# Moving parts built by VectorE alone, evictions spread over steps, and bias masks made as signs on ScalarE, in a hand-ordered transformer block

## The chip, the cores and the metric

The kernel runs on one core of one Trainium2 chip. The metric is the device time of one execution in microseconds (us). The core's engines are named as in the profile: PE (TensorE, matmuls), PEld (PE's weight loads), DVE (VectorE), ACT (ScalarE), POOL (GpSimd) and SP (SyncE, which here only issues DMAs). Each of them executes its own instructions strictly in order; semaphores hold an instruction back until what it needs is there. An engine's queue of issued DMAs appears with a q behind its name (ACTq, SPq). PSUM has eight banks of 128x512 float32, in which PE accumulates.

## The reference

One layer of a streaming encoder over 512 positions with 2048 channels, all in float32:

```python
h = rmsnorm(x, norm_gain)
proj = h @ w_in
(aq, ak, av, az, iq, ik, iw, rq, rk, rv, rz, ga, gb) = jnp.split(proj, SPLIT_POINTS, axis=-1)
...
# mixer A: for each query the 128 keys with the best index score
index = jnp.einsum('bqsh,bqh->bqs', jax.nn.relu(score), w_c)
_, sel = lax.top_k(index, topk)
bias = rel_table[t5_bucket(pos_sel - pos_c[:, :, None])]
logits = jnp.einsum('bqhd,bqkhd->bqkh', q_c, k_sel) * scale + bias
...
# mixer B: chunkwise retention over rq, rk (rotary) and rv, group norm
merged = sigmoid(ga) * (a_out @ w_a_out) + sigmoid(gb) * (b_out @ w_b_out)
r = x + merged @ w_o
return rmsnorm(r + (p_i @ w_ple) * sigmoid(r @ w_ple_gate), final_gain)
```

## The kernel before

**Precision.** A float32 product is made of three matmuls in the faster fp32r type: each operand is the sum of a high part (its value rounded to fp32r) and a low part (what is left), and high x high, high x low and low x high are accumulated. For a weight tile of 128x1024 (`wraw`, or `wt` for some), ACT makes the high part `wh` (line 153) and DVE subtracts it to get the low part `wl` (line 158). Every weight passes through ACT and DVE so, in `split_to`.

**Products in pairs.** Most of the projections are done two weight blocks at a time with a scheme of seven products in place of eight (Strassen's, in Winograd's form): `block_pair` and `block_wide_pair` set up the seven weight combinations. Some combinations are sums, which an accumulating DMA issued by POOL makes (line 119) or DVE (line 160). `gemm_pair` multiplies: for each of the seven products (units 0 to 6) there is a high run of eight matmuls 512 wide and a low run of eight matmuls 256 wide (line 283), in the order of `RUNS`: high 0, high 1, low 0, low 1, high 2, high 3, low 2, low 3, low 4, high 4, high 5, low 5, low 6, high 6. Four banks (`ps_p`, `ps_v`, `ps_q`, `ps_r`) accumulate. `SPLIT_AT` says ahead of which run a unit's split is recorded.

**The moving parts.** The other operand of those products is made once, from the normalised input `xn`, by `combos` (line 291). For each of eight steps `k` and each of seven combinations (`PRODUCTS`: s3, a11, a12, s4, s2, a22, s1) there is a tile of 128x512: its left half `LO` is the high part and comes from ACT (line 299), its right half `HI` is the low part. Four of the combinations need sums (`sums`, lines 310 to 316): four subtractions of 128x256. Before the change these are made by POOL (`adder=pool`), as are the low parts of s1, s4 and a22 (line 301); the other low parts are made by DVE. Tiles of the input carry names that begin with h in the profile (`hs`, `ha`), those of a later use, on `merged`, begin with m (`ms`). As all 56 tiles don't fit, twelve of them (`X_AWAY = 4` steps times three combinations) are stored to DRAM by SP when made and loaded again by `x_load` before they are needed.

**Passes of values.** `values` makes a half of rv: it multiplies 16 steps by four row tiles into four banks (`ps_vn`), in groups of three matmuls (lines 755 to 757). After it, `normal` (line 764) takes each bank out of PSUM with a scaling on ACT, and ACT issues the store of it (line 892). There are two such passes. They end at 148 and at 194.5 us. `values_pair` then makes both halves of av by the scheme of seven products, into banks `ps_vv`, `ps_vp`, `ps_vq` and `ps_vr` (two of each; lines 947 to 949); `copy` (ACT) and `out` take the banks out: `value_out` (line 896) makes the sum `av` on DVE (line 899), `split` makes the high part `avh` on ACT (line 734) and the low part `avl` on DVE (line 735), and ACT issues their stores 10 or 12 steps later (line 906). `last()` does so for four results at once at the end of the pair.

**Order.** No scheduler runs: the order of the instructions on each engine is the order in which the program records them. Each small group of matmuls (three in the passes, two in a gemm pair) ends with `step()`, a tick:

```python
def later(n, f):
    ...
    heapq.heappush(soon, (tick[0] + n, tick[1], f))

def step():
    tick[0] += 1
    while soon and soon[0][0] <= tick[0]:
        heapq.heappop(soon)[2]()
    f = todo.popleft() if todo else None
    if f is not None:
        f()
    elif bg and tick[0] % state["rate"] == 0:
        bg.popleft()()
```

Work for the other engines is so laid between the matmuls: what was put off with `later` falls due at its tick; else one entry of the list `todo` is recorded; else, each `rate`-th tick, one of the list `bg`. `BG_RATES` holds the rates of the stages. In `bg` stand, in this order, the steps of `combos`, the sixteen top-k rounds (`topk_round`, MAX8 at line 650 and MATCH_REPLACE8 at line 651, in three widths), and the bias masks.

**Around the change.** At 72 to 122 us the first rv pass and the index scores run (`index_score`: score matmuls at lines 610 and 611, relu on ACT at line 613, a weighted sum on DVE at line 620), with the split of the index queries (`iq_split`, lines 463 and 464) and the rotary tables (`f_turns` and `f_rope2`: `ang` on DVE at line 580, sine `st` and cosine `ct` on ACT at lines 587 and 590). The pair of av ends at 272 us and the first gemm pair begins (the gates; its `out` makes `e_t` at line 250 and `go` at line 967).

**Bias masks.** The bias depends on the bucket of the relative position. It is written as a first value plus a sum of differences, each times a mask "relative position at least threshold". A mask is 128 rows (32 buckets for each of four queries) by up to 512 keys in float16. DVE makes them with a comparison (line 666, 128 of them), `bias_mm` multiplies them with the table's differences `d2` (two float16 parts), and `bias_out` scales back by `d_back`.

**Space.** The U pool holds 69 tiles of 128x512 float32 (`U_BUFS`), given out in turn: a new tile takes the slot that was released, and its first writer waits until the slot's last reader (which may be a store) is done.

Of the kernel before, what the change touches and what calls it, by code (L numbers as in the profile page):

```python
# [9 lines left out]
F32 = mybir.dt.float32  # L10
# [25 lines left out]
def block_kernel(tc, xT, pT, posb, posq, w_in, w_v, w_ik, w_a, w_b, w_o, w_ple, w_gate,  # L36
# [4 lines left out]
    with contextlib.ExitStack() as ctx:  # L41
# [249 lines left out]
        def combos(lo, hi, name, keep=None, adder=dve, low={}):  # L291
# [5 lines left out]
            def parts(n, k, src, sign=1.0):  # L297
                t = U(name + n, F32R)
                act.activation(t[:, LO], src, AF.Copy, scale=sign)
                if sign > 0:  # L300
                    low.get(n, dve).tensor_sub(t[:, HI], src, t[:, LO].bitcast(F32))
# [81 lines left out]
        tb = cp.tile([128, 65], F32, name="tb")  # L383
# [150 lines left out]
        def f_pos():  # L534
# [11 lines left out]
            dve.max(d8, da)  # L546

# [6 lines left out]
        def f_table2():  # L554
# [7 lines left out]
            dve.tensor_scalar(d_back.bitcast(I32), e.bitcast(I32), 1.0, -14.0 * 2 ** 23, op0=OP.mult, op1=OP.add)  # L562
# [32 lines left out]
        todo.extend(N3 * 3 + [f_sum] + N3 * 3 + [f_rnat] + N3 * 3 + [f_bcast, None, f_keys1] + N3 * 3 + [f_keys2] + N3 * 2 + [f_keys3] + N3 * 2)  # L595
# [32 lines left out]

        for m in range(2):
            index_tile(m, ix[m])  # L630
# [28 lines left out]
        def bias_mask(b, i):  # L659

            t, gs = b
# [4 lines left out]
            dve.tensor_scalar(bias_e[b][:, ln * i:ln * i + ln], relf[:, :ln], thr[:, q:q + 1], None, op0=OP.is_ge)  # L666
# [28 lines left out]
        x_away = [(n, k) for k in range(X_AWAY) for n in PRODUCTS[4:]]  # L695
        hd = dp.tile([len(x_away), 128, L], F32, name="hd")
        x_at = {nk: hd[i] for i, nk in enumerate(x_away)}
        xn = {}

        def xn_load(k):  # L700
            for i in (k, k + 8):
                xn[i] = U("xn")
                sp.dma_start(xn[i], xT[:, i, :])

        def xn_norm(k):
            for i in (k, k + 8):
                dve.scalar_tensor_tensor(xn[i], xn[i], ng[:, i:i + 1], R["b"], op0=OP.mult, op1=OP.mult)

        Xh, h_step = combos(lambda k: xn[k], lambda k: xn[k + 8], "h", lambda n, k: x_at.get((n, k)), pool,
                            {n: pool for n in ("s1", "s4", "a22")})  # L710
# [172 lines left out]
        def x_load(s):  # L883
            if s >= KT - len(x_away) and x_wanted:
# [4 lines left out]
        for i in range(2):  # L889
            pss = values(u_rv[i], "rv", x_load if i else lambda s: None)  # L890
            for t, ps in enumerate(pss):
                act.dma_start(rd[i, t], normal(ps, "rv", t))
        state["rate"] = BG_RATES[2]


        def value_out(i, t, f, x, y):
# [8 lines left out]
            for j, v in vs:  # L905
                later(10 + 2 * (j % 2), lambda j=j, v=v: act.dma_start(vd[i, j], v))

        def values_pair(ids):
# [25 lines left out]
            for n, b in enumerate("vpqrpvp"):  # L934
# [20 lines left out]
        state["rate"] = BG_RATES[3]  # L955
# [29 lines left out]
        state["rate"] = BG_RATES[5]  # L985
# [408 lines left out]
BG_RATES = (2, 3, 5, 24, 16, 8)  # L1394
X_AWAY = 4
# [10 lines left out]
def _layout(x, p, positions, w_in, norm_gain, w_a_out, w_b_out, w_o, ret_gn_gain,  # L1406
# [88 lines left out]
```

## Time and profile before

| what | value |
|---|---|
| time, median of 3 runs | 1680.68 us |
| the runs | 1679.4, 1680.68 and 1682.84 us |
| profiled execution, its own time | 1680.43 us |
| profiled execution, its span | 1678.7 us |
| mean granted PE clock | 0.998 |
| DMA over the span | 204 GB/s, 343.26 MB |
| POOL's issue of accumulating DMAs of w_in (line 119) | 120, 106.1 us busy |
| wl on DVE (line 158) | 459, 565.4 us busy, 1241 ns each |
| wh on ACT (line 153) | 459, 474.3 us busy, 1043 ns each |

The profile has one profiled execution. In a row of instructions stand the start, the duration, the engine, the line, the operation, output <- inputs by the program's names, the shapes, the count, and in brackets how long the engine stood idle before and what released it. In a row of groups stand the count, the busy time, the mean ns of one, and the idle time ahead of them. PE's records overlap a little, as its matmuls are pipelined. The span is 1.7 us shorter than the profiled execution's own time.

### The profile page before, as it was taken

How to read it: one execution, taken by the hardware profiler on the slowest of the kernel's cores; microseconds unless marked ns; L12 is line 12 of the kernel's file. 1: busy time of each engine (PE TensorE's matmuls, PEld its weight loads, DVE VectorE, ACT ScalarE, POOL GpSimd, SP SyncE). 2: the span in 40 equal slices, each digit the busy share in tenths (PEclk: the TensorE clock that was granted, in tenths of full speed). 3: DMA queues.
4: the chain of work that ended last, by engine and by line, in shares of the span. 5: the costliest groups of instructions: out<-in, count | busy, mean ns of one | idle time of the engine just before them, and what ended most of it. 6: DMA issues, size and time to landing. Idle time of an engine off the chain costs nothing.

```text
span 1678.7 us, 24639 instructions
## 1 busy us (share of the span) xinstructions
PE 1660.2 (99%) x9160; PEld 1441.5 (86%) x9160; DVE 1300.1 (77%) x1984; ACT 880.0 (52%) x1296; POOL 284.3 (17%) x288
## 2 busy tenths in 40 slices
PE   9999999999999999999999999999999999999997
PEld 7988788888888888888888888888888888888896
DVE  7798988988988887887887777787668887864453
ACT  7465544555555555555555555566633445463342
POOL 2116611111111111111331111100000111112222
PEclk9999999999999999999999999999999999999999
DMA  7427989788788788788998888898466788733222
GB/s 288 127 91 236 321 234 268 174 218 218 181 210 220 178 232 230 168 229 227 248 235 219 218 223 218 247 373 284 162 210 193 196 216 218 208 108 101 88 63 101
DMA packets 125577, 343.26 MB, mean 204 GB/s; under 512 B 13713, under 2 KB 25873, under 8 KB 125457
## 3 DMA queue, kind: packets, MB, share of 16 engines
q1 hardware_dynamic: 90400, 235.22, 41.5%
q0 software_dynamic: 23680, 85.99, 28.1%
q10 hardware_dynamic: 11376, 20.47, 3.4%
q8 instruction: 72, 1.18, 0.3%
q14 instruction: 49, 0.39, 0.1%
HBM read 300.21 MB, written 41.42 MB: 204 GB/s over the span
## 4 chain that ended last, share of the span: by engine, by line
PE 89%; DVE 4%; ACT 2%; issue 2%; POOL 2%; DMA 1%; ACTq 0%; SPq 0%; POOLq 0%; DVEq 0%
PE ps_p L283 23%; PE ps_v L283 15%; PE ps_r L283 8%; PE ps_q L283 7%; PE ps_w L213 3%; PE ps_w L214 3%; PE ps_w L215 3%; PE ps_pg L215 3%; PE ps_pg L213 3%; PE ps_pg L214 3%; PE ps_iq L213 1%; PE ps_iq L215 1%; PE ps_iq L214 1%; DVE wl L158 1%; ACT wh L153 1%
## 5 line engine op out<-in xcount | busy, mean ns | idle before, releaser
L158 DVE TENSOR_TENSOR wl<-wraw,wh 128x1024 fp32r<-128x1024 f32 (+2 forms) x459 | 565.4, 1241 | 156.6 <-ACT wh L153 155.4
L153 ACT ACTIVATE wh<-wraw 128x1024 fp32r<-128x1024 f32 (+2 forms) x459 | 474.3, 1043 | 257.9 <-DVE wraw L160 120.3
L119 POOL DMA_DIRECT2D wraw<-w_in x120 | 106.1, 962 | 644.1 <-DVE mk L666 245.3
L283 PE MATMUL ps_p<-hs,wh 128*128 128x512 f32 x640 | 161.1, 394 | 0.0
L246 ACT ACTIVATE e<-ps_p 128x512 f32<-128x512 f32 x144 | 86.1, 598 | 136.7 <-PE ps_p L283 134.3
L283 PEld LDWEIGHTS ps_p<-hs,wh 128*128 128x128 f32 x640 | 114.9, 189 | 21.3 <-issue 0.7
L283 PE MATMUL ps_p<-hs,wl 128*128 128x256 f32 x640 | 92.1, 284 | 1.6 <-DVE wl L158 1.6
L283 PEld LDWEIGHTS ps_p<-hs,wl 128*128 128x128 f32 x640 | 83.0, 192 | 2.1 <-DVE wl L158 2.0
L283 PE MATMUL ps_r<-hs,wh 128*128 128x512 f32 x320 | 79.9, 392 | 1.3 <-ACT wh L153 1.3
L119 POOL DMA_DIRECT2D wraw<-w_o x24 | 21.1, 945 | 348.5 <-DVE wl L158 316.5
L283 PE MATMUL ps_q<-ha,wh 128*128 128x512 f32 x320 | 80.1, 392 | 0.0
L283 PE MATMUL ps_v<-ha,wh 128*128 128x512 f32 x320 | 80.0, 392 | 0.0
L283 PE MATMUL ps_p<-ha,wh 128*128 128x512 f32 x320 | 79.3, 390 | 0.0
L283 PE MATMUL ps_v<-hs,wh 128*128 128x512 f32 x320 | 79.0, 389 | 0.0
L215 PE MATMUL ps_pg<-rh,wl 128*128 128x512 f32 x192 | 74.8, 390 | 0.0
L214 PE MATMUL ps_pg<-rl,wh 128*128 128x512 f32 x192 | 74.7, 389 | 0.0
L213 PE MATMUL ps_pg<-rh,wh 128*128 128x512 f32 x192 | 74.7, 389 | 0.0
L967 DVE TENSOR_TENSOR go<-e_t 128x256 f32<-128x256 f32 x160 | 68.0, 425 | 6.8 <-DMA bd<-go 1.2
L283 PEld LDWEIGHTS ps_r<-hs,wh 128*128 128x128 f32 x320 | 59.6, 188 | 15.8 <-ACT wh L153 2.9
L283 PEld LDWEIGHTS ps_p<-ha,wh 128*128 128x128 f32 x320 | 59.9, 188 | 12.9 <-issue 0.5
L283 PEld LDWEIGHTS ps_v<-hs,wh 128*128 128x128 f32 x320 | 60.1, 188 | 12.5
L283 PEld LDWEIGHTS ps_v<-ha,wh 128*128 128x128 f32 x320 | 59.5, 188 | 12.1
(409 smaller groups left out, 3739.9 us busy)
## 6 DMA issues: line engine op xcount, KB each, us to landing
wraw<-w_in SPq DMA_DIRECT2D x172, 512.0 KB, 5.3
wraw<-w_in POOLq DMA_DIRECT2D x120, 512.0 KB, 8.0
wraw<-w_v SPq DMA_DIRECT2D x32, 512.0 KB, 4.2
wraw<-w_o SPq DMA_DIRECT2D x32, 512.0 KB, 4.8
wraw<-w_o POOLq DMA_DIRECT2D x24, 512.0 KB, 7.0
wraw<-w_gate SPq DMA_DIRECT2D x24, 512.0 KB, 4.0
wraw<-w_b SPq DMA_DIRECT2D x16, 512.0 KB, 5.9
wraw<-w_a SPq DMA_DIRECT2D x16, 512.0 KB, 4.1
```

Source lines behind the costliest of these rows:

```text
L119: pool.dma_start(out=view(raw_tiles[r], nk, cols), in_=src[:, k0:k0 + nk, :], accum_op=OP.add)
L153: act.activation(h, raw, AF.Copy)
L158: dve.tensor_sub(l, raw, h.bitcast(F32))
L213: pe.matmul(o, h[:, k, w], a, start=(s == order[0]), stop=False)
L214: pe.matmul(o, h[:, k, w], b, start=False, stop=False)
L215: pe.matmul(o, l[:, k, w], a, start=False, stop=(s == order[-1]))
L246: act.activation(E[n], src, AF.Copy)
L283: pe.matmul(o[:, c], w[:, k], X[PRODUCTS[n]][k][:, c], start=(n < 4 and first and k == 0), stop=(ended[n] == 16), skip_group_check=True)
L967: dve.tensor_add(o[:, q], c0, c1)
```

## The change

It has five parts.

1. `combos` loses its arguments `adder` and `low`: the four sums of a step and all low parts are made by DVE. That moves 56 operations of 128x256 from POOL to DVE.
2. The steps of `combos` start earlier: step 0 is recorded by `x_first`, from an entry of `todo`, one part each six ticks from tick 4 on; steps 1 to 7 stand in `bg` ahead of twelve empty entries (`X_PAUSE`) and the top-k rounds. `X_AWAY` is 5, so fifteen tiles are stored and loaded again; `x_load` begins earlier (`s > 2`) and goes on in the pair of values.
3. The results of an rv pass are taken out of PSUM, and stored, three ticks apart (`later(3 * t, ...)`). The last four of the pair of values are made at ticks 6, 9, 14 and 21 after its end, with their stores 18 or 20 ticks behind.
4. The bias masks are ACT's Sign of the relative position plus a negated threshold, so +1 or -1 in place of 1 or 0. The table's differences are halved (the exponent in `d_back`), its first value is set to the mean of first and last, the thresholds lie half-way between integers, and the table has one more column for the signs.
5. `BG_RATES` has five values: 2 till the rv passes are done, 5 in the pair of values, 24 behind it, 16 from the masks on, 8 at the end.

```diff
-        def combos(lo, hi, name, keep=None, adder=dve, low={}):
+        def combos(lo, hi, name, keep=None):
...
-                    low.get(n, dve).tensor_sub(t[:, HI], src, t[:, LO].bitcast(F32))
+                    dve.tensor_sub(t[:, HI], src, t[:, LO].bitcast(F32))
...
-                adder.tensor_sub(t2[:, LO], x[:, LO], x[:, HI])
-                adder.tensor_sub(t1[:, LO], x[:, HI], y[:, HI])
-                adder.tensor_sub(t1[:, HI], x[:, LO], t1[:, LO])
-                adder.tensor_sub(t2[:, HI], y[:, LO], t1[:, HI])
+                dve.tensor_sub(t2[:, LO], x[:, LO], x[:, HI])
+                dve.tensor_sub(t1[:, LO], x[:, HI], y[:, HI])
+                dve.tensor_sub(t1[:, HI], x[:, LO], t1[:, LO])
+                dve.tensor_sub(t2[:, HI], y[:, LO], t1[:, HI])
...
-            dve.tensor_scalar(thr, thr, tb[:, 64:65], None, op0=OP.add)
+            dve.tensor_scalar(thr, thr, tb[:, 64:65], -1.0, op0=OP.add, op1=OP.mult)
...
-            dve.tensor_sub(dl, tb[:, 0:32], tb[:, 32:64])
+            dve.scalar_tensor_tensor(dl, tb[:, 32:64], tb[:, 65:66], tb[:, 0:32], op0=OP.mult, op1=OP.add)
...
-            dve.tensor_scalar(d_back.bitcast(I32), e.bitcast(I32), 1.0, -14.0 * 2 ** 23, op0=OP.mult, op1=OP.add)
+            dve.tensor_scalar(d_back.bitcast(I32), e.bitcast(I32), 1.0, -15.0 * 2 ** 23, op0=OP.mult, op1=OP.add)
...
-        todo.extend(N3 * 3 + [f_sum] + N3 * 3 + [f_rnat] + N3 * 3 + [f_bcast, None, f_keys1] + N3 * 3 + [f_keys2] + N3 * 2 + [f_keys3] + N3 * 2)
+        todo.extend(N3 * 3 + [f_sum] + N3 * 3 + [f_rnat] + N3 * 3 + [f_bcast, lambda: x_first(), f_keys1] + N3 * 3 + [f_keys2] + N3 * 2 + [f_keys3] + N3 * 2)
...
+        def x_steps(k):
+            load = [lambda: xn_load(k + 1)] if k < 7 else []
+            return load + [lambda: xn_norm(k)] + [lambda i=i: h_step(k, i) for i in range(X_STEPS)]
+        def x_first():
+            for i, f in enumerate([lambda: xn_load(0)] + x_steps(0)):
+                later(4 + 6 * i, f)
...
-            dve.tensor_scalar(bias_e[b][:, ln * i:ln * i + ln], relf[:, :ln], thr[:, q:q + 1], None, op0=OP.is_ge)
+            act.activation(bias_e[b][:, ln * i:ln * i + ln], relf[:, :ln], AF.Sign, bias=thr[:, q:q + 1])
...
-        bg.append(lambda: xn_load(0))
-        for k in range(8):
-            if k < 7:
-                bg.append(lambda k=k: xn_load(k + 1))
-            bg.append(lambda k=k: xn_norm(k))
-            bg.extend([lambda k=k, i=i: h_step(k, i) for i in range(X_STEPS)])
-
-        bg.append(lambda: state.update(rate=BG_RATES[1]))
-        for r in range(16):
-            for t in range(1, NT):
-                bg.append(lambda r=r, t=t: topk_round(t, r == 15))
-        bg.append(lambda: state.update(rate=BG_RATES[4]))
+        rounds = [lambda r=r, t=t: topk_round(t, r == 15) for r in range(16) for t in range(1, NT)]
+        for k in range(1, 8):
+            bg.extend(x_steps(k))
+        bg.extend([lambda: None] * X_PAUSE)
+        bg.extend(rounds)
+        bg.append(lambda: state.update(rate=BG_RATES[3]))
...
         def x_load(s):
-            if s >= KT - len(x_away) and x_wanted:
+            if s > 2 and x_wanted:
...
-            pss = values(u_rv[i], "rv", x_load if i else lambda s: None)
-            for t, ps in enumerate(pss):
-                act.dma_start(rd[i, t], normal(ps, "rv", t))
+            for t, ps in enumerate(values(u_rv[i], "rv", x_load if i else lambda s: None)):
+                later(3 * t, lambda i=i, t=t, ps=ps: act.dma_start(rd[i, t], normal(ps, "rv", t)))
...
-                later(10 + 2 * (j % 2), lambda j=j, v=v: act.dma_start(vd[i, j], v))
+                later(lag + 2 * (j % 2), lambda j=j, v=v: act.dma_start(vd[i, j], v))
...
-            def out(f, b, n, i, half):
+            def out(f, b, n, i, half, at=0, lag=10):
                 for j in range(2):
-                    value_out(i, 2 * half + j, f, banks[b][j], E[n][j])
+                    later(at + at // 2 * j, lambda j=j: value_out(i, 2 * half + j, f, banks[b][j], E[n][j], lag))
...
-                out(dve.tensor_sub, "p", "pv", 1, 1)
-                out(dve.tensor_add, "r", "e3", 1, 0)
+                out(dve.tensor_sub, "p", "pv", 1, 1, 6, 18)
+                out(dve.tensor_add, "r", "e3", 1, 0, 14, 18)
...
+                    x_load(8 * n + s + 4)
...
-BG_RATES = (2, 3, 5, 24, 16, 8)
-X_AWAY = 4
+BG_RATES = (2, 5, 24, 16, 8)
+X_AWAY = 5
+X_PAUSE = 12
...
-    t = np.zeros((128, 65), f32)
+    t = np.zeros((128, 66), f32)
...
-            if b:
-                t[32 * q + b, 32 + 8 * q:40 + 8 * q] = tab[ROW[b - 1]]
-        t[32 * q:32 * q + 32, 64] = [-1e9] + THR[1:] + [1e9]
+            t[32 * q + b, 32 + 8 * q:40 + 8 * q] = tab[ROW[b - 1]]
+        t[32 * q:32 * q + 32, 64] = [-1e9] + [i - 0.5 for i in THR[1:]] + [1e9]
+        t[32 * q:32 * q + 32, 65] = [1.0] + [-1.0] * 31
```

More of the change, by code (lines that the diff above doesn't have):

```diff
@@ L382, in block_kernel @@
         posq_i = cp.tile([128, 128], I32, name="posq_i")
-        tb = cp.tile([128, 65], F32, name="tb")
+        tb = cp.tile([128, 66], F32, name="tb")
         ones = cp.tile([128, 128], F32, name="ones")
@@ L627, in index_tile, with xn_load, xn_norm @@
                     todo.append(lambda s=s, t=t: index_score(2 * m + s, ix[s], t))
+        x_away = [(n, k) for k in range(X_AWAY) for n in PRODUCTS[4:]]
+        hd = dp.tile([len(x_away), 128, L], F32, name="hd")
+        x_at = {nk: hd[i] for i, nk in enumerate(x_away)}
+        xn = {}
+        def xn_load(k):
+            for i in (k, k + 8):
+                xn[i] = U("xn")
+                sp.dma_start(xn[i], xT[:, i, :])
+        def xn_norm(k):
+            for i in (k, k + 8):
+                dve.scalar_tensor_tensor(xn[i], xn[i], ng[:, i:i + 1], R["b"], op0=OP.mult, op1=OP.mult)
+        Xh, h_step = combos(lambda k: xn[k], lambda k: xn[k + 8], "h", lambda n, k: x_at.get((n, k)))
+        def x_steps(k):
[4 more added lines that the diff above has]
+                later(4 + 6 * i, f)
         for m in range(2):
@@ L693, in bias_banks @@
                 bias_out(b, ps)
[L695 to L710, printed above, removed]
-        bg.append(lambda: xn_load(0))
-        for k in range(8):
-            if k < 7:
-                bg.append(lambda k=k: xn_load(k + 1))
-            bg.append(lambda k=k: xn_norm(k))
-            bg.extend([lambda k=k, i=i: h_step(k, i) for i in range(X_STEPS)])
-        bg.append(lambda: state.update(rate=BG_RATES[1]))
-        for r in range(16):
-            for t in range(1, NT):
-                bg.append(lambda r=r, t=t: topk_round(t, r == 15))
-        bg.append(lambda: state.update(rate=BG_RATES[4]))
+        rounds = [lambda r=r, t=t: topk_round(t, r == 15) for r in range(16) for t in range(1, NT)]
[4 more added lines that the diff above has]
+        bg.append(lambda: state.update(rate=BG_RATES[3]))
         banks = [(t, tuple(range(8 * t + g, 8 * t + g + n))) for t, n in reversed(tuple(enumerate((4, 2, 1, 1))))
@@ L954, in block_kernel @@
         values_pair(u_av)
-        state["rate"] = BG_RATES[3]
+        state["rate"] = BG_RATES[2]
         sgb, sga, mbs = (dp.tile([16, 128, L], F32, name=n) for n in ("sgb", "sga", "mbs"))
@@ L984, in block_kernel @@
                 gate_pair(u_g[n], to(d[m:m + 2], AF.Sigmoid))
-        state["rate"] = BG_RATES[5]
+        state["rate"] = BG_RATES[4]
         for n, u in enumerate(u_rz):
```

4 lines of the change are left out of this document (2 added, 2 removed).

## The prediction

> **What bounds the kernel now.** First the page: the busy shares and the chain that ended last.
>
> ```profile
> span 1678.7 us, 24639 instructions
> PE 1660.2 (99%) x9160; PEld 1441.5 (86%) x9160; DVE 1300.1 (77%) x1984; ACT 880.0 (52%) x1296; POOL 284.3 (17%) x288
> PE 89%; DVE 4%; ACT 2%; issue 2%; POOL 2%; DMA 1%; ACTq 0%; SPq 0%; POOLq 0%; DVEq 0%
> ```
>
> TensorE (PE) is busy 99% of the span, and 89% of the chain is its own work. The change removes no matmul, so all it can win is the time in which PE waits. That is the second view, the waits of PE; the columns are the total in us, the times and the longest.
>
> ```profile
> PE ps_b L1368 <- POOL rl L1364: 3.5, 1, 3.5
> PE ps_p L283 <- DVE wl L158: 1.6, 2, 1.3
> PE ps_vv L948 <- DVE wl L158: 1.5, 2, 0.8
> PE ps_vv L947 <- ACT wh L153: 1.4, 1, 1.4
> ...
> PE ps_r L283 <- ACT wh L153: 1.3, 3, 0.6
> ```
>
> The first is the end of the kernel and stays. The other four hold 1.6 + 1.5 + 1.4 + 1.3 = 5.8 us, 0.35% of the span; those left out hold 1.4 at the very start and less behind it. So 5.8 is the most that the change can win by taking waits away. What it can lose has no such bound: weights are split into wh on ScalarE (ACT) and wl on VectorE (DVE), and whatever stands in these queues ahead of a split can become a new wait of PE. So I looked for the places where the change puts work in front of one.
>
> **Part B: the evictions of the rv passes, −3.4 us.** The timeline of ACT at the end of the second rv pass, where the pair of av begins:
>
> ```profile
> 194.54 0.67 ACT L764 ACTIVATE rv<-ps_vn,r_nat 128x512 f32<-128x512 f32 x1
> 195.24 0.33 ACTq L892 DMA_DIRECT2D rd<-rv  x1
> ...
> 198.97 2.01 ACT L153 ACTIVATE wh<-wt 128x1024 fp32r<-128x1024 f32 x2 [0.40 <-ACT rv L764]
> ```
>
> And that of PE, with one of its waits:
>
> ```profile
> 194.46 0.39 PE L949 MATMUL ps_vv<-wh,hs 128*128 128x512 f32 x1
> 194.68 0.39 PE L947 MATMUL ps_vv<-wh,hs 128*128 128x512 f32 x1
> 195.86 0.50 PE L948 MATMUL ps_vv<-wl,hs 128*128 128x512 f32 x1 [0.79 <-DVE wl L158]
> ```
>
> Four evictions, each with its store issued behind it, fill ACT from 194.54 to 198.97; only then comes the next wh. DVE's wl needs that wh, and the three ps_vv waits above follow (1.4 + 1.5 = 2.9 us). In the changed order the evictions stand three steps (nine matmuls, some 2 us at the 0.23 from one matmul's start to the next) apart, and the wh stand between them; 0.67 + 0.33 us fits into 2 us. The three waits go. A stall costs a little more than the wait shown: at that pace the one at 195.86 follows the one at 194.68 by 0.95 us too much, of which 0.79 is called a wait. I add that 0.16 for each of the three: 2.9 + 0.5 = 3.4. Bounds: −2.9 to −3.6.
>
> **Part A: the moving parts on DVE alone, +2.6 us.** Per step k seven operations of 128x256 (four sums, three low parts) go from POOL to DVE, 56 in all, and step 0 is made some 64 us into the kernel instead of after 105 us. The prices on DVE, by shape, DVE's load in the two stretches concerned (columns: busy PE, PEld, DVE, ACT, POOL), and two rows of its timeline:
>
> ```profile
> L301 DVE TENSOR_TENSOR hs<-t,hs 128x256 fp32r<-128x256 f32 x16 | 13.9, 890 | 0.0
> L301 DVE TENSOR_TENSOR ms<-t,ms 128x256 fp32r<-128x256 f32 x32 | 12.0, 417 | 0.0
> 72.50:99.00 26.50, 26.50 (x151) 25.29 (x150) 23.20 (x50) 17.90 (x33) 0.00 (x0) 1.00 0.38 120
> 99.00:118.00 19.00, 19.00 (x92) 16.04 (x91) 18.82 (x29) 9.78 (x19) 4.00 (x4) 1.00 0.28 77
> ```
>
> ```profile
> 103.58 1.41 DVE L580 SCALAR_TENSOR_TENSOR ang<-kk,ang 128x512 f32<-128x512 f32 x2
> ...
> 110.84 2.37 DVE L580 SCALAR_TENSOR_TENSOR ang<-kk,ang 128x512 f32<-128x512 f32 x2
> ```
>
> The same operation takes 0.42 us alone (ms) and 0.89 beside POOL (hs); L580 shows it too, 1.41 and 2.37. So the moved operations cost 56 x 0.42 = 23 us, and 16 x 0.47 = 7.6 come back at the hs row, 0.96 at L580, more at others like it. Where they fall is what counts. From 72.5 to 99 DVE has 26.50 − 23.20 = 3.3 us free; step 0 brings 7 x 0.42 = 2.9 and the normalisation, two operations of 128x512 with two inputs, 1.41 like the pair at 103.58: 4.3 us, so 1.0 too much. From 99 to 118 it has 0.18 free; six operations of step 1 bring 2.5, and 0.96 comes back at L580: 1.4 too much (0.18 taken off). DVE is 2.4 us late at 118, and 0.7 more if a fifth of the free 3.3 falls between dependent instructions, where nothing fits. Who waits for that: ACT works in order, and its casts of the sums stand ahead of the following rows.
>
> ```profile
> 117.10 1.28 ACT L587 ACT_TABLE_LOAD   x1
> ...
> 119.79 0.72 ACT L590 ACTIVATE ct<-ang,cs 128x512 f32<-128x512 f32 x1 [0.76 <-DVE ang L588]
> 120.42 0.47 ACT L613 ACTIVATE relu<-ps_is 128x384 f32<-128x384 f32 x1
> ```
>
> ```profile
> 121.31 0.40 PE L610 MATMUL ps_is<-ikh,tz 128*128 128x512 f32 x1
> ```
>
> ACT's ct at L590 waits for DVE's ang, the relu at 120.42 stands behind it, and the matmul at 121.31 writes the bank which that relu empties at 120.89 (four of the eight banks hold rv until the pass ends). The slack is 0.4 to 0.5 us: 2.4 + 0.7 − 0.5 = +2.6. Bounds: 0, if what comes back for POOL's absence leaves ang no later, and +3.5, with all seven operations of step 1 and a little more idle in it.
> The Trainium skill, page "SBUF — State Buffer", section "Who interferes with whom", says that a DVE instruction with two SBUF inputs and a GpSimd instruction that reads SBUF exclude one another for the whole instruction. The pair 0.89 and 0.42 agrees, and by that rule alone the change repays DVE for much of what it brings, and A would be 0. The rows of 99 to 118 speak against that, since only 0.96 us of POOL's cost is seen there.
>
> **Part C: the evictions of the pair of av passes, +5.2 us.** This is the large term. The pair ends at 271.9, and the first gemm pair follows; its matmuls on PE, and the wait:
>
> ```profile
> 282.10 1.12 PE L283 MATMUL ps_r<-hs,wl 128*128 128x256 f32 x8
> 284.52 1.22 PE L283 MATMUL ps_p<-hs,wl 128*128 128x256 f32 x8 [1.30 <-DVE wl L158]
> ```
>
> Eight wide matmuls take 8 x 0.23 = 1.82 us, eight narrow ones half as long, some 0.93. So unit 4's low part, due at 282.10 + 0.93 = 283.0, came at 284.5: the wait of 1.3, with its restart 1.5. Today the four last evictions stand in one block at the head of the gemm pair and their stores block ACT; the change puts them at steps 6, 9, 14 and 21, stores 18 steps behind. That wait goes: −1.5. Without it unit 4's high part starts at 284.0, unit 5's high at 285.8 and its low at 287.6. The prices of what now stands in front of unit 5:
>
> ```profile
> L158 DVE TENSOR_TENSOR wl<-wraw,wh 128x1024 fp32r<-128x1024 f32 x3 | 3.6, 1216 | 0.0
> L735 DVE TENSOR_TENSOR avl<-av,avh 128x512 fp32r<-128x512 f32 x3 | 1.9, 682 | 0.0
> L246 ACT ACTIVATE e<-ps_p 128x512 f32<-128x512 f32 x144 | 86.1, 598 | 136.7 <-PE ps_p L283 134.3
> 276.68 0.49 ACTq L906 DMA_DIRECT2D vd<-av  x1
> ```
>
> DVE's changed order from 272.3 on: a top-k round of 512 (two passes of 512 at avl's 0.68, 1.4), three wl and one weight sum (4 x 1.22 = 4.9), four av and two avl (6 x 0.68 = 4.1), 10.4 in all, with 1.7 for the handovers to ACT and back: the last eviction, r's second half, is done at 284.4. ACT casts its avh (0.6), then issues three stores (0.33 as for rd, to 0.49 each, 1.25), then makes unit 5's wh (1.05): 287.3 where 285.8 was due, 1.5 late. DVE is later still. Its last avl goes into a slot of the U pool that an earlier avh leaves, whose store is issued just before, about 285.0; in the changed order that avl carries a wait for a DMA. DVE stands until the store has landed (L), then come avl 0.68, the output's e_t 0.68, go 0.42 (256 wide, as ms) and unit 5's wl 1.22: ready at 285.0 + L + 3.0 = 288.0 + L, due 287.6. PE waits 0.4 + L, in place of the 1.5. L from the issue-to-landing rows of such stores:
>
> ```profile
> vd<-avh ACTq DMA_DIRECT2D x2, 256.0 KB, 2.6
> vd<-avh ACTq DMA_DIRECT2D x1, 256.0 KB, 6.3
> vd<-avl ACTq DMA_DIRECT2D x1, 256.0 KB, 8.5
> ```
>
> They are 2.6 for two issued alone (234 us), 6.3 for the first of a batch behind two weight loads (267 us), 8.5 in a batch (278 us). Nearest is 6.3: a first store, weight loads about. C = 0.4 + 6.3 − 1.5 = +5.2; with the others +1.5 and +7.4.
> The Trainium skill, page "DMA: Bandwidth & Descriptors", section "Anatomy of one DMA — SWDGE (gpsimd) path", puts some 2.0 us, mostly the receipt of the write, on every transfer, and the bytes at 436 GB/s on top; an estimate from that page is 2.6 us here. The quiet store agrees, the other two do not; by the page's figure the sum below would be +0.7, 1681.1.
>
> **Part D: masks on ACT, 0.** The masks' source row, and a window of their stage:
>
> ```profile
> L666 DVE TENSOR_SCALAR mk<-relf,thr x128: 275/410/1461, 502.3 to 1039.4; 128x512 f16<-128x512 f32 x32, 128x384 f16<-128x384 f32 x32, 128x256 f16<-128x256 f32 x32, 128x128 f16<-128x128 f32 x32
> 800.00:840.00 40.00, 40.00 (x254) 34.21 (x253) 33.43 (x44) 22.51 (x30) 13.55 (x14) 1.00 0.97 264
> ```
>
> Some 128 x 0.41 = 52 us leave DVE, where PE waits for nothing (none of the waits lies there), so they buy nothing. On ACT each costs at most the 0.60 of a 512-wide pass: 77 us over 537 us; ACT has 17.5 of 40 us free. The free time is what hides it; without it, one mask in ten ahead of a late wh makes 12.8 x 0.6 = +7.7. The rest: three more parts are stored and loaded again, six DMAs of 256 KB more on SP; no wait of PE names a load behind the start, so 0, and at an issue of 0.33 each at most +2.0. The table's extra column and the idle slots ahead of the top-k rounds add no work on PE.
>
> **Sum:** 1680.4 (the profiled execution's own time) − 3.4 + 2.6 + 5.2 = 1684.8. The median of the runs is 1680.7, 0.3 above the profiled one, so nothing is added. About 0.2% (3.4 us) is what a measurement of this kernel can tell from no change.
>
> **The rivals.**
> R1, no new wait: the slot that avl takes is free in time and ang no later. −3.4 − 1.5 = 1675.5. For it: DVE's total falls by some 40 us (52 − 23 + 7.6 and more) and ACT has room. Against it: 0.18 us free from 99 to 118. This is the other side, faster.
> R2, A holds, the store doesn't hold DVE: −3.4 + 2.6 − 1.5 = 1678.1, no measurable change. For it: the two stores issued alone landed in 2.6, and a store issued earlier than 285.0 frees the slot in time.
> R3, C holds, A doesn't: −3.4 + 5.2 = 1682.2, no measurable change.
> R4, masks come ahead of wh: the one in ten above in place of A, −3.4 + 5.2 + 7.7 = +9.5, 1689.9. For it: ACT works in order; against it, 17.5 of 40 us free.
> R5, the upper prices: −2.9 + 3.5 + 7.4 = +8.0, 1688.4.
> That the change doesn't do what it says: the spread evictions may still be queued behind each other, since DVE's order, not the steps, sets when av is made; then B alone falls away and the sum is 1688.2, counted with R5.
>
> **How the numbers follow.** Forecast 0.46 (its own range 1682 to 1688; 0.38 of it slower, 0.08 within 0.2%), R1 0.19 faster, R2 0.08 and R3 0.09 the same, R4 0.06 and R5 0.12 slower. Faster 0.19, same 0.25, slower 0.56. The range runs from R1 (1675.5) to just above R5, 1690.
>
> **What would show it.** B: no ps_vv wait near 195 to 200. A: a wait of ps_is near 121 for relu, 2 to 3 us, with DVE full from 99 to 118. C: no wait for unit 4's wl, but one of PE for unit 5's wl near 288, 6 to 7 us, and DVE idle at an avl released by a DMA of vd. D: no PE wait from 502 to 1039. Wrong is the forecast if the wait at unit 5 is under 3 us or the score matmuls don't wait.

## The result, and the profile after

The changed kernel takes 1685.35 us (median of 14 runs) beside 1681.22 us of the kernel before (14 runs). The ratio is 1.0022, with an interval of 1.0014 to 1.0030: slower by 0.2%. 1684.8 us had been forecast. The profiled execution has a span of 1683.2 us beside 1678.7, 4.5 us more. The total came out as forecast, but the terms behind it did not: one was far too large, and one of nearly the same size was missing. That they cancel is luck.

First the page's two top rows, then the waits of PE (total us, times, longest), those at start and end left out:

```profile
span 1683.2 us, 24616 instructions
...
PE 1660.9 (99%) x9160; PEld 1440.9 (86%) x9160; DVE 1254.7 (75%) x1912; ACT 932.7 (55%) x1424; POOL 228.5 (14%) x232
```

```profile
PE ps_r L283 <- ACT wh L153: 3.4, 4, 1.7
PE ps_v L283 <- ACT wh L153: 2.5, 2, 1.6
PE ps_v L283 <- DVE wl L158: 1.6, 1, 1.6
...
PE ps_is L611 <- ACT relu L614: 1.3, 1, 1.3
...
PE ps_p L283 <- DVE wl L158: 0.8, 1, 0.8
PE ps_is L611 <- DVE tz L464: 0.4, 1, 0.4
```

DVE has 45 us less to do and ACT 53 us more, mostly the masks. Neither shows in the time; PE's busy time is the same. All that counts is in the second fence. Sorted by place, with the 0.16 us that each wait costs beside its length:

| place | waits before | waits after | change | forecast |
|---|---|---|---|---|
| B, 194 to 200 us | 2.9 in 3 | none | -3.4 | -3.4 |
| A, 101 and 121 us | none | 1.7 in 2 | +2.0 | +2.6 |
| C, 282 to 289 us | 1.3 in 1 | 2.5 in 2 | +1.3 | +5.2 |
| D, 480 to 1090 us | 0.7 in 2 | 4.9 in 4 | +4.5 | 0 |

The changes add up to +4.4, and the spans differ by 4.5. These are the waits of one profiled execution of each kernel; in the other traces the same place differs by up to 3 us, as the experiments show. A place is named by the start of the last matmul ahead of the wait; the row of the matmul that waited has a later time.

**Place A.** The timelines of ACT and of PE, and DVE's load from 99 to 118 us (columns as in the prediction):

```profile
117.98 1.22 ACT L299 ACTIVATE hs<-t 128x256 fp32r<-128x256 f32 x3 [3.10 <-DVE t L313]
119.10 0.37 ACT L614 ACTIVATE relu<-ps_is 128x256 f32<-128x256 f32 x1
119.48 1.28 ACT L588 ACT_TABLE_LOAD   x1
...
122.80 0.47 ACT L614 ACTIVATE relu<-ps_is 128x384 f32<-128x384 f32 x1
```

```profile
123.32 0.50 PE L611 MATMUL ps_is<-ikh,tz 128*128 128x512 f32 x1 [1.30 <-ACT relu L614]
```

```profile
99.00:118.00 19.00, 18.64 (x89) 15.44 (x88) 18.75 (x33) 8.21 (x17) 0.00 (x0) 1.00 0.19 56
```

ACT stands 3.1 us at the casts of step 1's sums, which DVE, full all the time, makes late. The table load comes 2.4 us later than before (119.48; it was 117.10), the relu too, and PE waits for it: the forecast wait, 1.3 long in place of 2 to 3. The other wait, 0.4 at 101 us for the split of the index queries (`tz`), had not been forecast.

**Place C.** DVE, the store that it waits for with its time to landing, and PE:

```profile
282.99 0.41 DVE L676 MATCH_REPLACE8 isc<-m,isc 128x256 f32<-128x256 f32 x1
285.74 0.69 DVE L739 TENSOR_TENSOR avl<-av,avh 128x512 fp32r<-128x512 f32 x1 [2.34 <-DMA vd<-avh]
```

```profile
282.65 0.33 ACTq L909 DMA_DIRECT2D vd<-avh  x1
```

```profile
vd<-avh ACTq DMA_DIRECT2D x1, 256.0 KB, 3.0
```

```profile
285.18 2.14 PE L283 MATMUL ps_v<-ha,wh 128*128 128x512 f32 x8 [0.87 <-ACT wh L153]
288.87 1.22 PE L283 MATMUL ps_v<-ha,wl 128*128 128x256 f32 x8 [1.55 <-DVE wl L158]
```

The last avl waits for the store that frees its slot, as forecast. But the store is issued at 282.65, not 285.0, and lands in 3.0 us, not 6.3. PE waits 0.87 for unit 5's wh and 1.55 for its wl.

**Place D.** Here the prediction had nothing. The rows of the masks and of MAX8 give their times, first and last:

```profile
L692 ACT ACTIVATE mk<-relf,thr x128: 384/554/737, 531.1 to 1055.5; 128x512 f16<-128x512 f32 x32, 128x384 f16<-128x384 f32 x32, 128x256 f16<-128x256 f32 x32, 128x128 f16<-128x128 f32 x32
```

```profile
L675 DVE MAX8 m<-isc x48: 417/554/689, 203.2 to 519.4; 128x8 f32<-128x256 f32 x16, 128x8 f32<-128x384 f32 x16, 128x8 f32<-128x512 f32 x16
```

The masks start at 531.1, not at 502.3. The top-k rounds ahead of them start later, so fewer of them fall into the stages with the quick rates, and three more go at one each 24 steps: in the recorded order the first bias bank stands at step 1206, before at 1126. The first four of the eleven pairs of banks come 80 steps later, the last six 40. The banks are so at other places within the gemm pairs of 56 steps. What this does at 941 us, in the order of time: SP's timeline, its wait, POOL's and ACT's rows:

```profile
907.53 0.33 SPq L132 DMA_DIRECT2D wraw<-w_in  x1
918.54 3.96 SPq L715 DMA_DIRECT2D scr<-bev  x4
922.61 1.33 SPq L132 DMA_DIRECT2D wraw<-w_in  x1
```

```profile
SPq L715 <- ACT bev L711: 10.6, 1, 10.6
```

```profile
933.36 0.88 POOL L119 DMA_DIRECT2D wraw<-w_in  x1 [10.40 <-issue]
```

```profile
942.12 1.06 ACT L153 ACTIVATE wh<-wraw 128x1024 fp32r<-128x1024 f32 x1 [5.42 <-DMA wraw<-w_in]
```

SP issues in order. It reaches the store of a bias bank and stands 10.6 us, till ACT has taken the bank out of PSUM; the weight loads behind it come out from 922.6 on and take some 10 us to land, POOL adds the second half of one at 933.36, that lands 8.7 us later, and ACT's wh stands 5.4 us for it. The hold alone is not the difference, though: in the kernel before SP stands 10.5 us ahead of the same stores (at 905 us), and no wait of PE follows. What differs is which loads are due behind it. That the hold makes this wait is read from the chain; no run takes the hold away and leaves all else. At 1071 us ACT's wh waits for the landing of a bias store. The chain there:

```profile
1062.84 8.45 DMA scr<-bev
...
1071.37 0.33 ACTq L981 DMA_DIRECT2D zd<-go  x1
1071.79 1.06 ACT L153 ACTIVATE wh<-wraw 128x1024 fp32r<-128x1024 f32 x1 [4.39 <-DMA scr<-bev]
```

A bias store takes 8.45 us to land, ACT's issue of a gate's store waits for that landing (the program makes it wait for the semaphore which that store raises, beside the one for its data), and the wh behind it is late.

### The profile page after: what moved, and what is told of

It reads as the page before. It is cut to its first block, busy times and chain, and to the rows that moved or that the text cites. A ratio compares the mean times of both kernels' runs of the same rounds, so it can differ in the third digit from the quotient of the medians.

```text
span 1683.2 us, 24616 instructions
## 1 busy us (share of the span) xinstructions
PE 1660.9 (99%) x9160; PEld 1440.9 (86%) x9160; DVE 1254.7 (75%) x1912; ACT 932.7 (55%) x1424; POOL 228.5 (14%) x232
## 5 line engine op out<-in xcount | busy, mean ns | idle before, releaser
L692 ACT ACTIVATE mk<-relf,thr 128x512 f16<-128x512 f32 (+3 forms) x128 | 70.8, 553 | 19.6 <-DVE go L971 11.9
```

Source lines behind the costliest of these rows:

```text
L692: act.activation(bias_e[b][:, ln * i:ln * i + ln], relf[:, :ln], AF.Sign, bias=thr[:, q:q + 1])
```

## The experiments

All ratios are to the kernel before, run on the same chips.

**Who makes the masks, and when.** The first two start from the changed kernel.

```diff
-            act.activation(bias_e[b][:, ln * i:ln * i + ln], relf[:, :ln], AF.Sign, bias=thr[:, q:q + 1])
+            dve.tensor_scalar(bias_e[b][:, ln * i:ln * i + ln], relf[:, :ln], thr[:, q:q + 1], None, op0=OP.is_ge)
...
```

> The changed kernel with its bias masks made by VectorE again, with the table as before; all else, the time of the masks too, stays. The changed kernel waits 5.6 us on TensorE in the stage of the masks at 707, 941, 950 and 1070 us, in places where the kernel before doesn't wait. Theory 1 (the masks stand in ScalarE's queue ahead of weight casts and evictions): these four waits go, about 1680 us. Theory 2 (the whole bias work comes 80 steps later and so at other places in the gemm pairs, where its stores meet the weight loads): the waits at 941 and 1070 stay whoever makes the masks, about 1685 us. The waits at 121 and 283 to 288 us stay in both.

Ratio 1.0011 (1.0002 to 1.0021). The waits of PE from 480 to 1090 us in this run:

```profile
PE ps_r L283 <- ACT wh L153: 2.2, 3, 1.6
PE ps_v L283 <- ACT wh L153: 1.9, 1, 1.9
PE ps_p L283 <- DVE wl L158: 0.2, 1, 0.2
```

4.3 of 4.9 us stay with the masks off ACT, the two large ones among them. Theory 1 falls for these. The time alone, between the two expectations, wouldn't have told.

```diff
         bg.append(lambda: state.update(rate=BG_RATES[3]))
+        bg.extend([lambda: None] * 2)
```

> The changed kernel with two empty slots of 16 steps ahead of the masks, which puts each bias bank one or two whole gemm pairs (56 steps each) after its place in the kernel before, so at the same place within a pair; the masks stay on ScalarE. Theory 1 (the masks in ScalarE's queue): waits of some 5 us stay in the stage, about 1685 us. Theory 2 (the place in the pair): they go, about 1680 us.

Ratio 0.9999 (0.9987 to 1.0010). The fifth of the eleven pairs of banks stands 72 steps after its old place, so not at the same place within a gemm pair; PE doesn't wait there. The waits at 707, 941, 950 and 1070 are gone, as theory 2 has it, but the profile has a new one at 679 us (3.1) and a small one after 840:

```profile
PE ps_r L283 <- ACT wh L153: 3.1, 1, 3.1
PE ps_v L283 <- DVE wl L158: 0.8, 1, 0.8
```

The chain behind the long one is of the kind seen at 941 us: SP stands at two stores ahead of weight loads, and ACT stands 3.9 us for a load that POOL issued at 661.87 and that landed 9.0 us later. And this wait costs more than its length. Behind it come eight wide matmuls, which elsewhere take some 2.0 us; then two windows, where the third number from the end is the granted clock of PE:

```profile
682.85 3.13 PE L283 MATMUL ps_r<-hs,wh 128*128 128x512 f32 x8 [3.12 <-ACT wh L153]
684.00:686.00 2.00, 2.00 (x7) 1.55 (x6) 1.97 (x3) 1.32 (x2) 0.00 (x0) 0.50 0.15 45
680.00:690.00 10.00, 7.15 (x40) 6.55 (x41) 8.18 (x11) 7.94 (x12) 0.00 (x0) 0.83 0.71 177
```

The clock is at half, and 10 us at 0.83 lose 1.7 us (an estimate from this row). The same stands, in the traces of these runs, behind each wait of 2.5 us or more between 20 and 1660 us: 1.7 or 1.8 us in this run, e3, e5, e8 and e10, 3.4 in e6 and e11. Behind shorter waits it stands there once (e1, 0.9 and 1.6 us close together at 283 to 289, 1.7 us); behind the same two waits in the changed kernel's own profile the clock stays at 1.00. The profiles of the kernel before and of the changed one have no such stretch, so the table above is free of it.

Theory 2 from the other side, in the kernel before:

```diff
         bg.append(lambda: state.update(rate=BG_RATES[4]))
+        bg.extend([lambda: None] * 5)
```

> The kernel before with five empty slots of 16 steps ahead of its masks: each bias bank stands at the step at which the changed kernel has it, and nothing else of the change is in it. If the place of the banks makes the waits in the stage of the masks, TensorE waits at about 937 and 1066 us as in the changed kernel (1.8 each), 3.5 to 4.6 us in all, ratio to the kernel before 1.002 to 1.003. If the masks on ScalarE make them, or the changed kernel's other moves do, nothing happens, ratio 1.000.

Ratio 1.0046 (1.0031 to 1.0061). PE's waits from 480 to 1090 us in this kernel, which has no other part of the change in it:

```profile
PE ps_r L283 <- ACT wh L153: 3.1, 4, 1.6
PE ps_v L283 <- ACT wh L153: 1.6, 1, 1.6
PE ps_p L283 <- DVE wl L158: 0.3, 1, 0.3
```

5.0 us in place of 0.7, and the two largest at 945 and 1075 us, with VectorE's masks. So the place of the banks makes them. The ratio is higher than these waits explain: the block of four evictions at 283 us waited 4.1 us in its profile, not 1.3, and behind it the clock is at half. Together that is 4.3 + 2.8 + 1.8 = 8.9 us, restarts left out, and the spans differ by 9.1. In the traces that have the banks at this place, the changed kernel's and six more, the waits of this stage add up to between 3.0 and 5.0 us.

The masks on ACT alone, at the old place, on top of the kernel with part B (e6, below), with the table's lines of the change:

```diff
-            dve.tensor_scalar(bias_e[b][:, ln * i:ln * i + ln], relf[:, :ln], thr[:, q:q + 1], None, op0=OP.is_ge)
+            act.activation(bias_e[b][:, ln * i:ln * i + ln], relf[:, :ln], AF.Sign, bias=thr[:, q:q + 1])
...
```

> The kernel before with the rv evictions spread and with the masks made by ScalarE as signs, at the steps at which they stand in the kernel before. If masks on ScalarE cost nothing where the banks stand well, the ratio is that of the kernel with the rv evictions alone, 0.997, and no wait over 1 us is in the stage of the masks. If they cost what the trace with masks on VectorE left open (0.8 us), 0.9975. Rival (the prediction's case of masks ahead of weight casts): several waits, 5 us and more, 1.000.

Ratio 0.9964 (0.9952 to 0.9976); in the stage of the masks PE waits 0.7 us, as in the kernel before. ScalarE's masks cost nothing that this run can tell (its interval is 2 us wide to each side) where the banks stand well.

**The rv evictions (B).** The kernel before with

```diff
-                act.dma_start(rd[i, t], normal(ps, "rv", t))
+                later(3 * t, lambda i=i, t=t, ps=ps: act.dma_start(rd[i, t], normal(ps, "rv", t)))
```

> The kernel before with the results of the rv passes taken out of PSUM three steps apart, and nothing else of the change. If part B of the prediction holds, the three waits at 194 to 200 us go and no new one comes: 3.4 us less, ratio 0.998. Rival: the wh is held by something else as well, or the later evictions hold the banks of the next pass, and no more than 1 us is won, ratio 0.9995 or more.

Ratio 0.9968 (0.9955 to 0.9981), and no wait of PE from 194 to 204 us. That is 5.4 us less (3.2 to 7.6), more than the 3.4 that was expected; where the rest comes from is not shown. The block at the end of the pair of av passes, untouched here, waited longer in this profile than in that of before (1.3):

```profile
PE ps_p L283 <- DVE wl L158: 2.8, 1, 2.8
```

With the 3.4 us that the clock loses behind it, this wait fits the profiled execution's 1680.40 us, the slowest of the six; the others took 1675.64 to 1678.78.

**The last four evictions (C).** In the changed kernel, the block again:

```diff
-                out(dve.tensor_sub, "p", "pv", 1, 1, 6, 18)
-                out(dve.tensor_add, "r", "e3", 1, 0, 14, 18)
+                out(dve.tensor_sub, "p", "pv", 1, 1)
+                out(dve.tensor_add, "r", "e3", 1, 0)
```

> The changed kernel with the last four evictions of the pair of av passes in one block again, stores 10 steps behind. If the spread evictions and the slot that waits for a store cost what the trace after shows, the waits at 283.7 and 286.7 us (1.0 + 1.7) go and the one of 1.5 at 282.7 comes back: 1.3 us less, about 1684 us. If the large price that the prediction put on the store were right, 5.2 us less, 1680 us. Rival: the block is worse now that other work has moved, 1687 us or more.

Ratio 1.0011 (1.0000 to 1.0022), which agrees with the expected 1.3 us less but does not show it, since the changed kernel's interval overlaps. The profile gives another reason than the expected one: the block's one wait is 2.5 us, as much as the two that went, with the clock at half behind it. What its span has less is in the masks' stage (waits of 3.0, not 4.9). So this run decides against the large price, no more.

The spread evictions with earlier stores:

```diff
-                out(dve.tensor_sub, "p", "pv", 1, 1, 6, 18)
-                out(dve.tensor_add, "r", "e3", 1, 0, 14, 18)
+                out(dve.tensor_sub, "p", "pv", 1, 1, 6, 10)
+                out(dve.tensor_add, "r", "e3", 1, 0, 14, 10)
```

> The changed kernel with the stores of the last four evictions 10 steps behind them instead of 18; the evictions stay spread. The first of these stores is issued some 3 us earlier, so that its slot is free when VectorE's last low part wants it. If that slot's store makes the waits at 283.7 and 286.7 us, the second goes (1.7 us) and VectorE doesn't stand at the last avl: about 1683.6 us, ratio to the kernel before 1.0012. If ScalarE's queue makes them (the earlier stores stand ahead of the same casts), both stay: 1.0022.

Ratio 1.0011 (1.0001 to 1.0021), and DVE goes through:

```profile
282.70 0.41 DVE L676 MATCH_REPLACE8 isc<-m,isc 128x256 f32<-128x256 f32 x1
283.03 0.68 DVE L739 TENSOR_TENSOR avl<-av,avh 128x512 fp32r<-128x512 f32 x1
```

No idle time stands before the avl now. Of C's two waits that for the wl is gone, and that for the wh is 0.5 in place of 0.9. The slot's store was the cause of DVE's stand and of the larger wait.

**The moving parts (A).** In the changed kernel, the parts on GpSimd again at their new, early time:

```diff
-                dve.tensor_sub(t2[:, LO], x[:, LO], x[:, HI])
+                adder.tensor_sub(t2[:, LO], x[:, LO], x[:, HI])
...
-        Xh, h_step = combos(lambda k: xn[k], lambda k: xn[k + 8], "h", lambda n, k: x_at.get((n, k)))
+        Xh, h_step = combos(lambda k: xn[k], lambda k: xn[k + 8], "h", lambda n, k: x_at.get((n, k)), pool,
+                            {n: pool for n in ("s1", "s4", "a22")})
```

> The changed kernel with the sums and three of the low parts of the input's moving parts on GpSimd again, at their new, earlier time. If VectorE's fuller queue is what makes the score matmuls wait, the waits at 101 and 121 us (0.5 + 1.5) go: 2.0 us less, about 1683.3 us. Rival: GpSimd's operations take longer and slow VectorE's beside them, so that the sums, and the casts on ScalarE behind them, come later still: 1687 us or more.

Ratio 1.0032 (1.0020 to 1.0043): slower. The wait at 101 goes and that at 121 falls to 0.6, but the pair of av passes now waits for its parts:

```profile
PE ps_vp L952 <- ACT wh L153: 2.2, 1, 2.2
PE ps_vp L953 <- DVE wl L158: 0.8, 1, 0.8
```

The empty slots ahead of step 1:

```diff
+        bg.extend([lambda: None] * X_PAUSE)
         for k in range(1, 8):
             bg.extend(x_steps(k))
-        bg.extend([lambda: None] * X_PAUSE)
```

> The changed kernel with its twelve empty slots ahead of step 1 of the moving parts instead of ahead of the top-k rounds: VectorE has none of step 1's work from 99 to 118 us, all else is recorded in the same order and number. If this work makes the score matmul at 121 us wait, that wait of 1.5 goes and the one at 101 (0.5, step 0's work) stays: 1.5 us less, ratio to the kernel before 1.0013. Rival: the parts come late for the pair of av passes at 194 us, which then waits: 1.0022 or more.

Ratio 1.0047 (1.0032 to 1.0062). The wait at 121 goes and that at 101 stays, as expected of the cause, but the rival's price is higher:

```profile
PE ps_vv L951 <- ACT wh L153: 1.5, 1, 1.5
PE ps_vv L952 <- DVE wl L158: 1.5, 2, 0.8
```

Step 1's work in that stretch does make the score matmul wait; moved as a block it comes late for the pair. These waits are not the whole of the higher time: the profile also has one of 2.6 us near 950, with the clock at half behind it, and one of 1.9 at the start.

The parts on VectorE alone, at the old time, on e6:

```diff
-        Xh, h_step = combos(lambda k: xn[k], lambda k: xn[k + 8], "h", lambda n, k: x_at.get((n, k)), pool,
-                            {n: pool for n in ("s1", "s4", "a22")})
+        Xh, h_step = combos(lambda k: xn[k], lambda k: xn[k + 8], "h", lambda n, k: x_at.get((n, k)))
```

> The kernel before with the rv evictions spread and with the sums and all low parts on VectorE, at the old, later time. If VectorE's queue has room in the second rv pass (GpSimd no longer slows it), nothing changes: 0.997. If it is full there, the last steps' parts or the weights' splits come late for the pair of av passes near 194 us, 2 to 5 us of new waits: 0.998 to 1.000. That would say why the changed kernel starts the parts earlier, at the price of the waits at 101 and 121.

Ratio 0.9970 (0.9958 to 0.9981), that of e6; PE waits neither near 121 nor near 194. The stretch from 118 to 194 us in e6 and then in this kernel:

```profile
118.00:194.00 76.00, 76.00 (x341) 63.07 (x340) 68.78 (x79) 43.75 (x87) 53.03 (x57) 1.00 0.82 259
```

```profile
118.00:194.00 76.00, 76.00 (x340) 62.94 (x339) 63.71 (x133) 44.05 (x87) 5.45 (x6) 1.00 0.81 254
```

And the row of the low parts in e6 and here (minimum, median, maximum in ns):

```profile
L301 DVE TENSOR_TENSOR hs<-t,hs x16: 412/956/965, 117.6 to 190.4; 128x256 fp32r<-128x256 f32 x16
```

```profile
L301 DVE TENSOR_TENSOR hs<-t,hs x32: 354/418/426, 118.1 to 190.0; 128x256 fp32r<-128x256 f32 x32
```

DVE takes over POOL's operations and is busy 5 us less, since those it already had run faster without POOL beside them: the hs at 0.42 us, not 0.96, and the eleven wl of `wraw` in this stretch at 1.23, not 1.59.

**The parts that pay, together.** First the kernel before with part B (the edit of e6) and the spread of part C, stores 10 steps behind:

```diff
-                    value_out(i, 2 * half + j, f, banks[b][j], E[n][j])
+                    later(at + at // 2 * j, lambda j=j: value_out(i, 2 * half + j, f, banks[b][j], E[n][j], lag))
...
-                out(dve.tensor_sub, "p", "pv", 1, 1)
-                out(dve.tensor_add, "r", "e3", 1, 0)
+                out(dve.tensor_sub, "p", "pv", 1, 1, 6, 10)
+                out(dve.tensor_add, "r", "e3", 1, 0, 14, 10)
```

> The kernel before with the rv evictions spread and with the last four evictions of the pair of av passes at steps 6, 9, 14 and 21, stores 10 steps behind: no slot there waits for a fresh store in this order. Moving parts, masks and rates are those before. The kernel with the rv evictions alone waited 3.0 us at 279 us for the block of four. If the block and its stores make that wait, it goes: 1.5 to 3.0 us less than that kernel, ratio to the kernel before 0.995 to 0.996, the fastest so far. Rival: the spread evictions and stores delay the casts of units 4 and 5 as in the changed kernel: ratio 0.997 or more.

Ratio 0.9958 (0.9947 to 0.9970), 1675.89 us: the lowest median of all. Its waits from 270 to 310 us:

```profile
PE ps_v L283 <- ACT wh L153: 0.5, 1, 0.5
PE ps_r L283 <- ACT wh L153: 0.5, 1, 0.5
```

Then the changed kernel with both mends, the edits of e2 and e7:

```diff
+        bg.extend([lambda: None] * 2)
...
-                out(dve.tensor_sub, "p", "pv", 1, 1, 6, 18)
-                out(dve.tensor_add, "r", "e3", 1, 0, 14, 18)
+                out(dve.tensor_sub, "p", "pv", 1, 1, 6, 10)
+                out(dve.tensor_add, "r", "e3", 1, 0, 14, 10)
```

> The changed kernel with both mends, stores 10 steps behind and two empty slots ahead of the masks. By the two single runs, waits of 1.9 us at 283 to 287 and of 4 to 5 us in the stage of the masks go: 1685.4 less 6, about 1679.5, ratio 0.999; the waits at 101 and 121 stay. Rival: the wait of 3.3 us at 679 that the run with empty slots showed belongs to that place of the banks and comes in each run: ratio 1.001.

Ratio 0.9987 (0.9978 to 0.9996), 1679.64 us, as expected. The wait of 3.1 us at 679 is in its profile again, with 3.4 us lost to the clock behind it. That execution took 1684.05 us, the longest of its twelve; the shortest took 1678.88. In e2 too the profiled execution, 1685.93 us, is one of the longest (1680.82 to 1686.04). That the wait comes in some executions only would fit, but is only argued.

## Why the prediction was right, and where it was not

**The time** was right to 0.6 us by luck: two errors nearly cancel, as C's term was 3.9 us too large and D's 4.5 too small. The direction is owed to them too: with A, B and C at their measured sizes and D at 0 the sum is −3.4 + 2.0 + 1.3 = −0.1, no change.

**B was right** in place, cause and waits: three waits, 2.9 us and their restarts, gone in the changed kernel and in e6. The time of e6 fell by 5.4 us (3.2 to 7.6), so the size by the time is larger than 3.4, or at the edge of it.

**A was right in its wait and near in size** (2.0 for 2.6, of which 0.5 is the wait at 101 that it did not have), and half right in what it blamed. Its step "56 x 0.42 = 23 us, and 16 x 0.47 = 7.6 come back" undercounted what comes back: in e12 the moved operations lower DVE's busy time by 5 us from 118 to 194 and make no wait. The rule cited from the Trainium skill, page "SBUF — State Buffer", section "Who interferes with whom", is borne out by the two hs rows above. At the old time A is 0 by the runs, as it would be by that rule. The price needs both the early time and DVE as maker. Step 1 stands in a stretch that had 0.18 us free: e8 takes it out and the wait at 121 goes. With POOL as maker at the early time (e4) the wait at 101 goes and that at 121 falls to 0.6, at the price of new waits in the pair. And the early start wasn't needed: e12 starts late, and nothing waits.

**C had the right mechanism and a wrong size.** The step that failed is L, "Nearest is 6.3": the store took 3.0 us. The quiet row's 2.6 was the nearest, since the spread leaves this store the first in the queue, with no batch around it. With the lower bound C would have been +1.5; measured is +1.3. The estimate from the Trainium skill, page "DMA: Bandwidth & Descriptors", section "Anatomy of one DMA — SWDGE (gpsimd) path", was 2.6 as well, and the trace agrees within 0.4 here; in bursts it doesn't (8.1 to 8.5 for these stores before). That section's figures are for DMAs that GpSimd issues, while this store is issued by ScalarE. The sum also took the block's wait from one profile, 1.3 us. In other kernels that keep the block it was 1.9 (e12), 2.5 (e3), 2.7 (e10), 2.8 (e6) and 4.1 (e5). Against a block of that length the spread's 2.5 us cost nothing even with its slot, and without it (e9, 1.0 us) it wins some 2 us by the waits; by the times, 0.9958 and 0.9968 with overlapping intervals, e9 and e6 can't be told apart. Last, the sum priced a wait at little more than its length. The one it forecast, 0.4 + 6.3, is longer than all those behind which the clock was at half here, and a price for that was left out without a reason.

**D failed in one sentence**: "The table's extra column and the idle slots ahead of the top-k rounds add no work on PE." They add none; but together with the new rates and the earlier parts they move the banks behind them in the list, the first by 80 steps and those at the two largest waits by 40, and a bank's place within a pair decides whether these waits come. That they come through SP's queue, where loads stand behind the bank's stores, is read from the chain at 941 us; the one at 1071 comes through a store's landing on ACT. The prediction counted the masks' cost on ACT, in which e10 finds none and which R4 priced at 7.7, and not the moves of the stores. e5 gets the same two waits from five empty slots alone.

**R1's time** (1675.5, no new wait) is about what e9 reaches (1675.89). Its ratio stands for 7.1 us (5.0 to 8.9): the 5.8 us of waits that the prediction called the most to be won lies in that interval, and is not shown to be a bound. e9 gets there without the changes to parts, masks and rates.

Open: why the block's wait varies between 1.3 and 4.1 us, among the kernels and perhaps among the executions of one, why the wait at 679 us comes, and what makes e6's time fall by more than its waits.

## What to carry to other kernels

Where work is laid between matmuls by a step count, an edit early in the list moves everything behind it: compare, for each later group, the step at which it stands, and what stands behind its stores in the queue that issues them. For a buffer that a store must free, take the landing time of a store in the same situation (first in a quiet queue, or in a burst), not the median. Where a stall is long, look at the granted clock behind it as well as at its length. A small sum that comes out right proves its terms only if each place is measured by itself.

## What the hardware showed that was not expected

Behind each wait of TensorE of 2.5 to 4.1 us in the traces named above its granted clock was at or near 0.50 for some microseconds, and 1.7 to 3.4 us more were lost. An issue of a store on ScalarE stood 4.4 us for the landing of another array's store (8.45 us), whose semaphore the program makes it wait for, with the weight cast behind it. SyncE stood 10.6 us at one store while weight loads waited behind, and 10.5 in the kernel before, where it cost nothing. And giving VectorE more operations made it less busy: 68.8 us in 118 to 194 fell to 63.7, since what it had already ran faster: a 128x256 subtraction takes 0.42 us with GpSimd silent and 0.96 (median) beside it.
